# Retention's products with q in the tiles of v, and the squares of norm 2 behind two K tiles of fill

## The chip, the cores and the metric

The kernel runs on one core of a Trainium2 chip. The metric is the device time of one execution in microseconds; the time before the change is the median of three runs. A profiled execution was taken beside them.

## The reference

One step of a decoder trunk with one layer: 256 prompt positions and 8 samples of one position each share the weights, 264 columns in all. Everything is float32, and the model dimension is 2048.

```
h = rmsnorm(x, norm1_g) * (1 + scale1) + shift1
q, k, v, gr, u, ga, gb = split(h @ w_in)        # q, k rotated; 8 heads, dqk 256, dv 512
# retention of a sample, head by head, with its own state S (256 x 512):
S_new = gamma_h * S + outer(k, v)               # an output
o     = q @ S_new
y_a = (group_norm(o) * gn_g * silu(gr)) @ w_proj_a
mixed = sigmoid(ga) * y_a + sigmoid(gb) * y_b   # y_b: pooled branch
x = x + gate1 * (mixed @ w_out)
h2 = rmsnorm(x, norm2_g) * (1 + scale2) + shift2
x = x + gate2 * ((silu(a) * b) @ w_down)        # a, b: causal conv of h2 @ w_up
```

The six shifts, scales and gates are one product each of silu(c) with w_mod ("modulation"). The prompt's retention is done with scores and a state of its own. A final norm follows.

## The kernel before, in words

**Weights.** All weights stream from memory once. A chunk is 4 K tiles of 128 by 256 outputs (512 KB). SP's queue loads it into a ring of six raw tiles (L203), ScalarE casts it to `whi` (L214), VectorE subtracts to get the remainder `wlo` (L215), each in a ring of three, and TensorE runs 24 products: hi with hi, hi with lo, lo with hi (L228 to L236). These products go through `mm` (L194), which ties every product behind the one before it, so from the end of the start stage on their order on TensorE is the order written in the program. Everything else is laid out by the framework's planner, which simulates a timeline and gives each engine one list of instructions. `behind(a, b)` (L183) tells the planner alone that a comes after b on their engine.

**A head.** While the chunks of head h+1 run (q, k, then half of the output projection of head h-1, v, the other half, v, gate), the retention of head h is spread between them: `main` has 32 chunks (24 in head 0; in head 7 the gate ga takes the place of the next head), and `spread` (L90) puts step j of n behind chunk ceil(32(j+1)/n). Before the change there are 18 steps: rows of v, scores, values and keys; samples 0 and 1; prompt outputs; samples 2 and 3; prompt states; samples 4 and 5; modulation with the first sums; samples 6 and 7; modulation with the second sums; sample outputs, centring, gate. The first sums so come behind chunk 22 and the second behind chunk 27 (16 and 20 in head 0).

**A sample** (`sample`, L652): GpSimd's queue loads S (512 KB, ring of four, shared in head 7 with the stores of ga); VectorE's shuffle spreads the row of v over the partitions into `vb` (ring of two); ScalarE scales S by gamma; VectorE adds k times v in two halves; GpSimd's queue stores S. The product with q goes to a tile of its own, `qt` (ring of four): ScalarE multiplies half 0 by q (L665), VectorE adds half 1 (L666). `sample_q` (L670) sums over the partitions on TensorE for four samples at a time, with products of 32 columns at four tile positions. One step of modulation, which loads four raw tiles of 512 KB on SP's queue and runs eight products, goes in front of each.

**Norm 2.** The output projection ends with its eighth group (L850). Squares of the groups 0 to 6 are summed and enter the norm's sum `pn_n2` early; the squares of the last two tiles (`square_part`, L791) are taken behind their residual and enter it by two products that are not tied. Nine K tiles of a modulation product (`gt2`, L854, four products each, weights loaded ahead) are the fill while the norm is worked out: square root on ScalarE, reciprocal over 264 columns on VectorE (L341), the samples' columns of h2 by three GpSimd products and a split, the prompt's by VectorE and ScalarE tile by tile (`modulated`, L344). Then the up projection starts.

Of the kernel before, what the change touches and what calls it, by code (L numbers as in the profile page):

```python
# [20 lines left out]
F32 = mybir.dt.float32  # L21
# [4 lines left out]
P = 128  # L26
# [3 lines left out]
TP = 256  # L30
NS = 8
T = TP + NS
H = 8
DQK = 256
DV = 512
# [51 lines left out]
GAMMA = constants()[3]  # L87
# [13 lines left out]
def run(steps):  # L101
    for step in steps:
        step()


def call(f, *args):
    return lambda: f(*args)


def together(*steps):  # L110
    return lambda: run(steps)
# [18 lines left out]
def build(ctx, tc, a):  # L130
    nc = tc.nc
    ve, sc, te, sy, gp = nc.vector, nc.scalar, nc.tensor, nc.sync, nc.gpsimd
# [50 lines left out]
    def behind(ins, first):  # L183

        tc.add_manual_dep(ins.ins, first.ins.name, mybir.DependencyInfo(
            mybir.DependencyClass.NoSync, mybir.DependencyReason.DATA), reason="issue order")


    mark = {}
# [21 lines left out]
    def split_loaded(w, name, nk):  # L211
        hi = wts.tile([P, 4, 256], F32R, tag="whi", name=f"wh_{name}", bufs=3)[:, 0:nk, :]
        lo = wts.tile([P, 4, 256], F32R, tag="wlo", name=f"wl_{name}", bufs=3)[:, 0:nk, :]
        c = sc.copy(out=hi, in_=w)  # L214
        t = ve.tensor_tensor(out=lo, in0=w, in1=hi.bitcast(F32), op=ALU.subtract)  # L215
        if name == "st0_0":
            behind(c, mark["ms"])
            behind(t, mark["hm"])
        if name == "st0_4":
            behind(c, mark["hi"])  # L220
            behind(t, mark["lo"])
        return hi, lo
# [114 lines left out]
    def rstd_from(pn, name):  # L337

        r = keep.tile([P, T], F32, tag="rstd", name=f"rstd_{name}")
        mark[name] = sc.activation(out=r, in_=pn[:, :T], func=AF.Sqrt, bias=eps[:, 0:1], scale=1.0 / D)  # L340
        ve.reciprocal(out=r, in_=r)  # L341
        return r

    def modulated(x, r, isc, ish, k0, nk, xh, xl, name):  # L344
# [228 lines left out]
    def retention(h, mods):  # L573

        q, k, v, gr = raw_q[h], raw_k[h], raw_v[h], raw_gr[h]
        st = {}
# [75 lines left out]
        def sample(b):  # L652

            s = hp.tile([P, 2, DV], F32, tag="S", name=f"S{h}_{b}", bufs=4)
            gp.dma_start(out=s, in_=a["state_ret"][b, h].rearrange("(d p) v -> p d v", p=P))
            vb = hp.tile([P, DV], F32, tag="vb", name=f"vb{h}_{b}", bufs=2)
            ve.stream_shuffle(out=vb, in_=st["vsr"], mask=[b] * 32)
            sc.mul(out=s, in_=s, mul=GAMMA[h])
            for d in range(2):
                ve.scalar_tensor_tensor(out=s[:, d, :], in0=vb, scalar=k[:, d, TP + b:TP + b + 1],  # L660
                                        in1=s[:, d, :], op0=ALU.mult, op1=ALU.add)
            gp.dma_start(out=a["rs"][b, h].rearrange("(d p) v -> p d v", p=P), in_=s)

            t = hp.tile([P, DV], F32, tag="qt", name=f"qt{h}_{b}", bufs=4)
            sc.mul(out=t, in_=s[:, 0, :], mul=q[:, 0, TP + b:TP + b + 1])  # L665
            ve.scalar_tensor_tensor(out=t, in0=s[:, 1, :], scalar=q[:, 1, TP + b:TP + b + 1], in1=t,  # L666
                                    op0=ALU.mult, op1=ALU.add)
            st["qt", b] = t

        def sample_q(half):  # L670

# [33 lines left out]
        def gate():  # L705
# [16 lines left out]
            sample_rows, scores, together(call(values, 0), call(values, 1), keys),  # L722
            call(sample, 0), call(sample, 1), together(call(prompt_out, 0), call(prompt_out, 1)),
            call(sample, 2), call(sample, 3), together(call(prompt_state, 0), call(prompt_state, 1)),
            call(sample, 4), call(sample, 5), together(*mods[0:1], call(sample_q, 0)), call(sample, 6),
            call(sample, 7), together(*mods[1:2], call(sample_q, 1)),
            sample_out, centre, gate,
        ]

# [61 lines left out]
    def square_part(kt, b, dst, pool, norm, t0, t1):  # L791

        q = pool.tile([P, T], F32, tag="t1", name=f"rql_{norm}_{b}_{t0}", bufs=2)[:, 0:t1 - t0]
        sc.activation(out=q, in_=dst[:, kt, t0:t1], func=AF.Square)
        te.matmul(out=pns[norm][:, t0:t1], lhsT=ones, rhs=q, start=False, stop=b == 1, skip_group_check=t0 > 0)

    def residual(acc, xin, gate, g, dst, pool, norm):

        for b in range(2):
            residual_part(acc, xin, gate, 2 * g + b, b, dst, 0, T)  # L800
            if g == 7:
                square_part(2 * g + b, b, dst, pool, norm, 0, T)
        k = slice(2 * g, 2 * g + 2)
        if g == 0:
            sums[norm] = pool.tile([P, 2, T], F32, tag="ssum", name=f"ssum_{norm}", bufs=1)
            sc.activation(out=sums[norm], in_=dst[:, k, :], func=AF.Square)
        elif g < 7:
            q = pool.tile([P, 2, T], F32, tag="t2", name=f"rsq_{norm}_{g}", bufs=4)
            sc.activation(out=q, in_=dst[:, k, :], func=AF.Square)
            ve.tensor_tensor(out=sums[norm], in0=sums[norm], in1=q, op=ALU.add)  # L810
        if g == 6:
            warm_sqrt(norm, sums[norm][:, 0, 0:1])
            pns[norm] = psx(f"pn_{norm}")
            for b in range(2):
                te.matmul(out=pns[norm][:, :T], lhsT=ones, rhs=sums[norm][:, b, :], start=b == 0, stop=False)

    sums, pns = {}, {}
    x1 = midp.tile([P, KT, T], F32, tag="ya", name="x1")
    with tc.tile_pool(name="res", bufs=2) as rp:
        def load_ahead(src, name):  # L820
            return loaded.pop(0)

        loaded = []

        def loads_ahead(g):

            for n in range(2):
                w = rp.tile([P, 4, 256], F32, tag="rawx", name=f"wm2_ahead_{g}_{n}", bufs=KT)
                if g > 1:
                    hold(w[:, 0, 0:1], x1[:, 2 * g - 3, 0:1])  # L830
                gp.dma_start(out=w, in_=a["w_mod2"][2 * (GT2 - 2) + n, g])
                loaded.append(w)

        c_late = rp.tile([P, KT, 32], F32, tag="c_late", name="c_late", bufs=1)
        gt2, _ = mod2_steps(GT2)
        xbs = {}

        def load_x(g):
            xbs[g] = rp.tile([P, 2, T], F32, tag="xb", name=f"xb{g}")
            sy.dma_start(out=xbs[g], in_=a["xT"][:, 2 * g:2 * g + 2, :])  # L840

        def use_wo(g, acc):
            residual(acc, xbs[g], GT1, g, x1, rp, "n2")
            sy.dma_start(out=dram["x1"][:, 2 * g:2 * g + 2, :], in_=x1[:, 2 * g:2 * g + 2, :])

        for gs in ([0, 1], [2], [3], [4], [5], [6], [7]):
            for g in gs:
                load_x(g)
                loads_ahead(g)
            run(gemm(a["w_out"], gs, m_hi, m_lo, KT, "wo", use_wo, apart=gs == [7]))  # L850

        hold(c_late[:, 0, 0:1], x1[:, 12, 0:1])
        gp.tensor_copy(out=c_late, in_=csil)
        for kt in range(9):  # L854
            gt2(kt, 1, load_ahead if kt < KT // 2 else raw_chunk, c_late)
        r2 = rstd_from(pns["n2"], "n2")
    h2_hi = acts.tile([P, KT, T], F32R, tag="a_hi", name="h2_hi")
# [187 lines left out]
```

## Time and profile before

| | before |
|---|---|
| median of 3 runs (lowest to highest), us | 2294.38 (2294.06 to 2294.73) |
| profiled execution: its own time / its span, us | 2300.14 / 2298.4 |
| mean granted TensorE clock | 0.993 |
| TensorE busy / VectorE / ScalarE / GpSimd | 98% / 65% / 47% / 9% |
| read and written, over the span | 243 GB/s |

The span goes from the first to the last instruction of the profiled execution; times in the rows are from the span's start. Busy times count instructions that run; a matmul overlaps the next one, so a busy TensorE is not one at its peak. An instruction's idle time before it is in brackets, with what ended it.

### The profile page before, as it was taken

How to read it: one execution, taken by the hardware profiler on the slowest of the kernel's cores; microseconds unless marked ns; L12 is line 12 of the kernel's file. 1: busy time of each engine (PE TensorE's matmuls, PEld its weight loads, DVE VectorE, ACT ScalarE, POOL GpSimd, SP SyncE). 2: the span in 40 equal slices, each digit the busy share in tenths (PEclk: the TensorE clock that was granted, in tenths of full speed). 3: DMA queues.
4: the chain of work that ended last, by engine and by line, in shares of the span. 5: the costliest groups of instructions: out<-in, count | busy, mean ns of one | idle time of the engine just before them, and what ended most of it. 6: DMA issues, size and time to landing. Idle time of an engine off the chain costs nothing. (4 is left out here: it accounts for less than half of the span.)

```text
span 2298.4 us, 44797 instructions
## 1 busy us (share of the span) xinstructions
PE 2252.8 (98%) x18432; PEld 2148.8 (93%) x18432; DVE 1504.3 (65%) x2152; ACT 1088.6 (47%) x1364; POOL 218.2 (9%) x386
## 2 busy tenths in 40 slices
PE   8999999999999999999999999999999999999998
PEld 6898998898999999999999989989999999999998
DVE  6666676585758686867676568576666666654444
ACT  4333354355554545454545454454444444444343
POOL 0000222011101010101010101111000010000000
PEclk9999999999999999999999999999999999999999
DMA  9777867897877787878787879856666666666662
GB/s 334 246 263 268 278 193 264 296 343 285 283 257 272 255 286 257 294 260 298 240 294 238 285 229 347 301 164 186 199 183 214 192 207 212 184 191 190 187 193 98
DMA packets 168253, 561.13 MB, mean 244 GB/s; under 512 B 18448, under 2 KB 28752, under 8 KB 168048
## 3 DMA queue, kind: packets, MB, share of 16 engines
q1 hardware_dynamic: 144048, 474.08, 62.4%
q0 software_dynamic: 23568, 83.73, 10.1%
q8 instruction: 144, 2.36, 0.4%
q10 hardware_dynamic: 432, 0.46, 0.1%
q14 instruction: 61, 0.50, 0.1%
HBM read 509.82 MB, written 48.38 MB: 243 GB/s over the span
## 5 line engine op out<-in xcount | busy, mean ns | idle before, releaser
L196 PE MATMUL acc_up<-h_hi,wh_up 128*128 128x264 f32 x1408 | 400.8, 285 | 1.5 <-ACT h_hi L225 1.5
L196 PE MATMUL acc_up<-h_lo,wh_up 128*128 128x264 f32 x1408 | 400.1, 284 | 0.7 <-DVE h_lo L226 0.7
L196 PE MATMUL acc_up<-h_hi,wl_up 128*128 128x264 f32 x1408 | 399.6, 284 | 0.0
L196 PE MATMUL acc_in<-h_hi,wh_in 128*128 128x264 f32 x1344 | 390.3, 290 | 3.2 <-ACT wh_in L214 3.2
L196 PE MATMUL acc_in<-h_hi,wl_in 128*128 128x264 f32 x1344 | 384.6, 286 | 6.8 <-DVE wl_in L215 6.8
L196 PE MATMUL acc_in<-h_lo,wh_in 128*128 128x264 f32 x1344 | 384.7, 286 | 0.0
L215 DVE TENSOR_TENSOR wl_up<-w_up,wh_up 128x1024 fp32r<-128x1024 f32 x176 | 216.0, 1227 | 182.0 <-ACT wh_up L214 181.9
L215 DVE TENSOR_TENSOR wl_in<-w_in,wh_in 128x1024 fp32r<-128x1024 f32 x168 | 207.6, 1237 | 154.6 <-ACT wh_in L214 154.6
L214 ACT CAST wh_up<-w_up 128x1024 fp32r<-128x1024 f32 x176 | 184.6, 1049 | 252.3 <-issue 148.7
L214 ACT CAST wh_in<-w_in 128x1024 fp32r<-128x1024 f32 x168 | 175.7, 1048 | 207.9 <-PE acc_in L196 79.4
L196 PEld LDWEIGHTS acc_in<-h_hi,wh_in 128*128 128x128 f32 x1344 | 255.4, 190 | 17.3 <-ACT wh_in L214 13.5
L196 PEld LDWEIGHTS acc_up<-h_hi,wh_up 128*128 128x128 f32 x1408 | 265.4, 189 | 5.8 <-ACT h_hi L225 2.5
L196 PEld LDWEIGHTS acc_up<-h_lo,wh_up 128*128 128x128 f32 x1408 | 265.7, 189 | 0.9 <-DVE h_lo L226 0.9
L196 PEld LDWEIGHTS acc_up<-h_hi,wl_up 128*128 128x128 f32 x1408 | 265.0, 188 | 0.0
L196 PEld LDWEIGHTS acc_in<-h_hi,wl_in 128*128 128x128 f32 x1344 | 254.8, 190 | 9.2 <-DVE wl_in L215 9.1
L196 PEld LDWEIGHTS acc_in<-h_lo,wh_in 128*128 128x128 f32 x1344 | 255.5, 190 | 0.5
L196 PE MATMUL acc_st<-h_hi,wh_st 128*128 128x264 f32 x704 | 202.1, 288 | 1.0 <-ACT h_hi L358 1.0
L196 PE MATMUL acc_st<-h_hi,wl_st 128*128 128x264 f32 x704 | 200.4, 286 | 1.9 <-DVE wl_st L215 1.8
L196 PE MATMUL acc_st<-h_lo,wh_st 128*128 128x264 f32 x704 | 200.2, 285 | 0.0
L196 PE MATMUL acc_dn<-f_lo,wh_dn 128*128 128x264 f32 x680 | 192.9, 284 | 0.0
L196 PE MATMUL acc_dn<-f_hi,wl_dn 128*128 128x264 f32 x680 | 192.8, 284 | 0.0
L196 PE MATMUL acc_dn<-f_hi,wh_dn 128*128 128x264 f32 x680 | 192.8, 284 | 0.0
(262 smaller groups left out, 5346.4 us busy)
## 6 DMA issues: line engine op xcount, KB each, us to landing
wm<-in_w_mod SPq DMA_DIRECT2D x176, 512.0 KB, 6.3
w_up<-in_w_up SPq DMA_DIRECT2D x176, 512.0 KB, 3.7
w_in<-in_w_in SPq DMA_DIRECT2D x168, 512.0 KB, 4.9
w_dn<-in_w_down SPq DMA_DIRECT2D x88, 512.0 KB, 3.6
S<-in_state_ret POOLq DMA_DIRECT2D x64, 512.0 KB, 7.0
out_rs<-S POOLq DMA_DIRECT2D x64, 512.0 KB, 5.6
w_pa<-in_w_proj_a SPq DMA_DIRECT2D x64, 512.0 KB, 4.2
w_st<-in_w_in SPq DMA_DIRECT2D x66, 384.0 KB, 4.5
```

Of the source, the lines that this page charges most:

```text
L196: ins = te.matmul(**kw)
L214: c = sc.copy(out=hi, in_=w)
L215: t = ve.tensor_tensor(out=lo, in0=w, in1=hi.bitcast(F32), op=ALU.subtract)
```

## The change

- The product with q is written into the sample's `vb` tile; the ring of `vb` has six tiles, and `qt` is gone (six tiles in both).
- The shuffle and the scaling of S are tied behind the subtraction and the cast of the latest split in front of them in the program.
- The first sums, with their step of modulation, stand behind sample 4 instead of sample 5; an empty step stands in front of the second sums, so there are 19 steps. The first sums come behind chunk 19 (14 in head 0), the second behind chunk 27 (21 in head 0), samples 0 to 7 behind chunks 7, 9, 12, 14, 17, 21, 22 and 24 (before: 8, 9, 13, 15, 18, 20, 24 and 25).
- The last squares of norm 2 are taken in the program behind two K tiles of the fill, and their two products go through `mm`.
- Norm 2's reciprocal is done in two parts, the eight columns of the samples first.

```diff
@@ -213,6 +213,7 @@
         lo = wts.tile([P, 4, 256], F32R, tag="wlo", name=f"wl_{name}", bufs=3)[:, 0:nk, :]
         c = sc.copy(out=hi, in_=w)
         t = ve.tensor_tensor(out=lo, in0=w, in1=hi.bitcast(F32), op=ALU.subtract)
+        mark["split"] = c, t
         if name == "st0_0":
             behind(c, mark["ms"])
             behind(t, mark["hm"])
@@ -338,7 +339,9 @@
 
         r = keep.tile([P, T], F32, tag="rstd", name=f"rstd_{name}")
         mark[name] = sc.activation(out=r, in_=pn[:, :T], func=AF.Sqrt, bias=eps[:, 0:1], scale=1.0 / D)
-        ve.reciprocal(out=r, in_=r)
+
+        for t in (slice(TP, T), slice(0, TP)) if name == "n2" else (slice(0, T),):
+            ve.reciprocal(out=r[:, t], in_=r[:, t])
         return r
 
     def modulated(x, r, isc, ish, k0, nk, xh, xl, name):
@@ -653,19 +656,19 @@
 
             s = hp.tile([P, 2, DV], F32, tag="S", name=f"S{h}_{b}", bufs=4)
             gp.dma_start(out=s, in_=a["state_ret"][b, h].rearrange("(d p) v -> p d v", p=P))
-            vb = hp.tile([P, DV], F32, tag="vb", name=f"vb{h}_{b}", bufs=2)
-            ve.stream_shuffle(out=vb, in_=st["vsr"], mask=[b] * 32)
-            sc.mul(out=s, in_=s, mul=GAMMA[h])
+            vb = hp.tile([P, DV], F32, tag="vb", name=f"vb{h}_{b}", bufs=6)
+
+            behind(ve.stream_shuffle(out=vb, in_=st["vsr"], mask=[b] * 32), mark["split"][1])
+            behind(sc.mul(out=s, in_=s, mul=GAMMA[h]), mark["split"][0])
             for d in range(2):
                 ve.scalar_tensor_tensor(out=s[:, d, :], in0=vb, scalar=k[:, d, TP + b:TP + b + 1],
                                         in1=s[:, d, :], op0=ALU.mult, op1=ALU.add)
             gp.dma_start(out=a["rs"][b, h].rearrange("(d p) v -> p d v", p=P), in_=s)
 
-            t = hp.tile([P, DV], F32, tag="qt", name=f"qt{h}_{b}", bufs=4)
-            sc.mul(out=t, in_=s[:, 0, :], mul=q[:, 0, TP + b:TP + b + 1])
-            ve.scalar_tensor_tensor(out=t, in0=s[:, 1, :], scalar=q[:, 1, TP + b:TP + b + 1], in1=t,
+            sc.mul(out=vb, in_=s[:, 0, :], mul=q[:, 0, TP + b:TP + b + 1])
+            ve.scalar_tensor_tensor(out=vb, in0=s[:, 1, :], scalar=q[:, 1, TP + b:TP + b + 1], in1=vb,
                                     op0=ALU.mult, op1=ALU.add)
-            st["qt", b] = t
+            st["qt", b] = vb
 
         def sample_q(half):
 
@@ -722,8 +725,8 @@
             sample_rows, scores, together(call(values, 0), call(values, 1), keys),
             call(sample, 0), call(sample, 1), together(call(prompt_out, 0), call(prompt_out, 1)),
             call(sample, 2), call(sample, 3), together(call(prompt_state, 0), call(prompt_state, 1)),
-            call(sample, 4), call(sample, 5), together(*mods[0:1], call(sample_q, 0)), call(sample, 6),
-            call(sample, 7), together(*mods[1:2], call(sample_q, 1)),
+            call(sample, 4), together(*mods[0:1], call(sample_q, 0)), call(sample, 5), call(sample, 6),
+            call(sample, 7), together(), together(*mods[1:2], call(sample_q, 1)),
             sample_out, centre, gate,
         ]
 
@@ -792,14 +795,15 @@
 
         q = pool.tile([P, T], F32, tag="t1", name=f"rql_{norm}_{b}_{t0}", bufs=2)[:, 0:t1 - t0]
         sc.activation(out=q, in_=dst[:, kt, t0:t1], func=AF.Square)
-        te.matmul(out=pns[norm][:, t0:t1], lhsT=ones, rhs=q, start=False, stop=b == 1, skip_group_check=t0 > 0)
+        (mm if norm == "n2" else te.matmul)(
+            out=pns[norm][:, t0:t1], lhsT=ones, rhs=q, start=False, stop=b == 1, skip_group_check=t0 > 0)
 
     def residual(acc, xin, gate, g, dst, pool, norm):
 
         for b in range(2):
             residual_part(acc, xin, gate, 2 * g + b, b, dst, 0, T)
             if g == 7:
-                square_part(2 * g + b, b, dst, pool, norm, 0, T)
+                squares.append(call(square_part, 2 * g + b, b, dst, pool, norm, 0, T))
         k = slice(2 * g, 2 * g + 2)
         if g == 0:
             sums[norm] = pool.tile([P, 2, T], F32, tag="ssum", name=f"ssum_{norm}", bufs=1)
@@ -814,7 +818,7 @@
             for b in range(2):
                 te.matmul(out=pns[norm][:, :T], lhsT=ones, rhs=sums[norm][:, b, :], start=b == 0, stop=False)
 
-    sums, pns = {}, {}
+    sums, pns, squares = {}, {}, []
     x1 = midp.tile([P, KT, T], F32, tag="ya", name="x1")
     with tc.tile_pool(name="res", bufs=2) as rp:
         def load_ahead(src, name):
@@ -852,6 +856,9 @@
         hold(c_late[:, 0, 0:1], x1[:, 12, 0:1])
         gp.tensor_copy(out=c_late, in_=csil)
         for kt in range(9):
+            if kt == 2:
+                run(squares)
+                squares.clear()
             gt2(kt, 1, load_ahead if kt < KT // 2 else raw_chunk, c_late)
         r2 = rstd_from(pns["n2"], "n2")
     h2_hi = acts.tile([P, KT, T], F32R, tag="a_hi", name="h2_hi")
```

## Rows read from the trace of the kernel before

**Rows 1.** The page, busy time of TensorE: us (share) xinstructions.

```profile
PE 2252.8 (98%) x18432; PEld 2148.8 (93%) x18432; DVE 1504.3 (65%) x2152; ACT 1088.6 (47%) x1364; POOL 218.2 (9%) x386
```

**Rows 2.** TensorE's waits, 475 to 562 us: total us, times, longest.

```profile
PE mean_mu L693 <- DVE s_mu L691: 1.6, 1, 1.6
PE acc_in L196 <- DVE wl_in L215: 1.2, 2, 0.7
PE osp L684 <- ACT qs L679: 0.8, 1, 0.8
```

**Rows 3.** TensorE's waits, 562 to 1228 us.

```profile
PE acc_in L196 <- DVE wl_in L215: 4.9, 7, 0.8
PE acc_in L196 <- ACT wh_in L214: 1.8, 2, 1.1
```

**Rows 4.** TensorE's waits, 1228 to 1372 us.

```profile
PE qp L196 <- DVE qt L666: 3.5, 1, 3.5
```

**Rows 5.** Windows: us, PE PEld DVE ACT POOL (x), granted clock, DMA share, GB/s.

```profile
546.00:554.00 8.00, 6.91 (x31) 6.23 (x32) 7.07 (x11) 4.89 (x6) 0.00 (x0) 0.57 0.82 287
1102.00:1107.00 5.00, 5.00 (x30) 5.00 (x31) 2.45 (x2) 2.62 (x4) 0.00 (x0) 0.66 0.86 293
1327.00:1335.00 8.00, 6.76 (x24) 4.25 (x23) 4.18 (x6) 3.06 (x5) 0.72 (x1) 0.57 1.00 370
1501.00:1506.00 5.00, 4.03 (x20) 3.83 (x21) 5.00 (x14) 2.68 (x7) 0.00 (x0) 0.66 0.52 204
```

**Rows 6.** Timeline of ScalarE, from 1098.55: start, length, instruction, idle before it.

```profile
1098.55 1.06 ACT L658 ACTIVATE S<-S 128x1024 f32<-128x1024 f32 x1 [1.55 <-DMA S<-in_state_ret]
1099.52 1.03 ACT L214 CAST wh_in<-w_in 128x1024 fp32r<-128x1024 f32 x1
```

**Rows 7.** The tiles of S, who waited for them: us, times.

```profile
  ACT wh_in L214: 9.3, 7
```

**Rows 8.** The tiles qt: min/median/max ns, first and last start; what they waited for.

```profile
L665 ACT ACTIVATE qt<-S,q x64: 705/718/738, 486.3 to 1327.3; 128x512 f32<-128x512 f32 x64
...
  PE qp L196: 5.4, 7
```

**Rows 9.** Transfers, 624 to 634 (first row), then 640 to 650: KB, us to landing.

```profile
w_in<-in_w_in SPq DMA_DIRECT2D x3, 512.0 KB, 3.7
...
DMA packets 1075, 3.95 MB, mean 395 GB/s; under 512 B 111, under 2 KB 111, under 8 KB 1074
...
w_in<-in_w_in SPq DMA_DIRECT2D x2, 512.0 KB, 9.5
```

**Rows 10.** Windows, columns as in rows 5.

```profile
600.00:612.00 12.00, 12.00 (x98) 11.84 (x98) 10.26 (x16) 4.96 (x7) 2.72 (x4) 1.00 0.93 312
684.00:720.00 36.00, 36.00 (x285) 34.92 (x284) 36.00 (x65) 18.96 (x25) 7.69 (x11) 1.00 0.73 248
```

**Rows 11.** Timeline of ScalarE in head 7, at 1321.84.

```profile
1321.84 1.04 ACT L214 CAST wh_ga<-w_ga 128x1024 fp32r<-128x1024 f32 x1 [7.90 <-DMA w_ga<-in_w_in]
```

**Rows 12.** Timeline of norm 2, from 1490.61.

```profile
1490.61 4.50 PE L196 MATMUL mp<-wm_ahead,c_late 128*32 128x512 f32 x40
...
1491.38 0.17 DVE L789 TENSOR_TENSOR x<-x,xb 128x8 f32<-128x8 f32 x1
1491.55 0.73 ACT L794 ACTIVATE rql_n<-x 128x264 f32<-128x264 f32 x2
...
1495.03 1.16 PE L795 MATMUL pn_n<-rql_n,ones 128*128 128x264 f32 x4
...
1496.23 0.48 ACT L340 ACTIVATE rstd_n<-pn_n,eps 128x264 f32<-128x264 f32 x1 [3.95 <-PE pn_n L795]
1496.74 1.80 DVE L341 RECIPROCAL rstd_n<-rstd_n 128x264 f32<-128x264 f32 x1 [3.84 <-ACT rstd_n L340]
...
1501.31 0.39 PE L196 MATMUL acc_up<-h_hi,wh_up 128*128 128x264 f32 x1 [1.54 <-ACT h_hi L225]
...
1502.36 0.59 PE L196 MATMUL acc_up<-h_lo,wh_up 128*128 128x264 f32 x1 [0.67 <-DVE h_lo L226]
```

## The prediction

> **What bounds the kernel now.** I read the page's busy times first: TensorE is busy for 98% of the span [rows 1]. There is no slower engine to relieve; the change can only take away TensorE's idle time, and the time at the lower clock that follows it. So the second view is TensorE's waits, stage by stage, and the third the granted clock around the longest of them. The chain of waits tells the same: from norm 2 on it is nearly all matmuls.
>
> The eight heads run from 475 to 1372 us. In head 0 TensorE waits 1.6 us for the sums of the mean, 1.2 us for remainders of weights and 0.8 us for the copy in front of the transposes [rows 2]. In heads 1 to 6 it waits 4.9 us (7 times) for remainders and 1.8 us (twice) for casts of weights [rows 3]. In head 7 it waits 3.5 us for one product with q [rows 4]. The clock was granted at 0.57 for 8 us in head 0, at 0.66 for 5 us in head 5, at 0.57 for 8 us in head 7 and at 0.66 for 5 us at norm 2 [rows 5]. Each begins just after a cluster of these waits; the two levels are 1.2 and 2.4 GHz, and a stretch of w us at a granted share c loses w(1-c): 3.4, 1.7, 3.4 and 1.7 us.
>
> Why the weights are late is on ScalarE, not in the transfer of weights. At 1098.55 a scaling of a sample's state S starts, after 1.55 us of waiting for that S to land, and only behind it, at 1099.52, the cast of the weights for which TensorE then stands idle [rows 6]. These are the next head's samples 0 to 3, which the planner put into the end of this head, far ahead of their use. All over the run casts of wh_in had 9.3 us of idle ended by an instruction on S in front of them, 7 times [rows 7]. Their products of samples 4 to 7 wait 5.4 us (7 times) on ScalarE for the first half of the sums on TensorE, since the ring of product tiles holds four [rows 8]; so the S tiles come free only then, and four loads of S start at once, in the same stretch as 2 MB of modulation weights. There a load of w_in lands after 9.5 us, against 3.7 us ten microseconds earlier [rows 9].
>
> **The change, part by part.** No matmul, and no instruction per sample, goes or comes; one reciprocal is split.
>
> (a) Six tiles for v and product. Products of samples 4 and 5 lose the wait for the first sums; those of 6 and 7 now wait for them earlier, at the shuffle that fills the tile. The product on ScalarE (0.72 us) now overwrites v, so it waits for both sums into S instead of the first, and VectorE's second half of it for that [rows 8].
>
> (b) The first half of the sums, with one step of modulation, goes from behind chunk 22 of 32 to behind chunk 19 (head 0: 16 to 14 of 24); the second stays behind 27 (head 0: 20 to 21). The step issues four loads of 512 KB on SP's queue, so they pass in front of the loads of three chunks; the two bursts are eight chunks apart instead of five. At chunk 19 the first four products are long done: they lie before the second group of projections.
>
> (c) The ties. The scaling of S stays behind the cast of the chunk in front of it in the program, the shuffle behind its subtraction. The next head's scalings can't be put in front of this head's casts any more. That is what each stall above needs. What it costs: ScalarE gets them, 4 x 1.06 us, in the stretch where VectorE is full (36.00 of 36 us) but ScalarE has 18.96 of 36 us busy [rows 10]; it fits. Behind a tied shuffle that waits for the first sums stand VectorE's next subtractions. Sample 6 comes behind chunk 22, whose weights can be split only when TensorE has left chunk 19 (three buffers), just ahead of the sums; so the wait is short, and the next subtraction is needed two chunks later.
>
> Gains in the heads. Head 0: 1.6 + 1.2 + 0.8 less 0.8, because sums and transposes are now one chunk apart and the copy between them can still show, plus 3.4 of clock: 6.2 us. Heads 1 to 6: 4.9 + 1.8 + 1.7 of clock = 8.4 us. Head 7: ends 0 and 3.5 + 3.4 = 6.9 us. There the cast itself started only at 1321.84, after 7.90 us in which ScalarE waited for its transfer [rows 11], and the tiles of S are shared with the gate's stores, whose order in the ring changes; the nearest row is that wait for a transfer, which the change doesn't shorten for sure, so I take half, 3.4.
>
> New waits can't be read here. They end below at 0 (nothing more to gain: TensorE has no idle in the full stretch) and above at one short stall per head, as the longest of those seen for weights, 0.75 us, by eight heads: 6.0 us. As VectorE has no spare time there, and the waits of (a) fall on it, I take the upper end, 6.0.
>
> (d) Norm 2. TensorE's fill starts at 1490.61: 40 instructions, then the sums of the last squares at 1495.03, then the rest of it, and idle from 1499.77 to 1501.31 (1.54 us) and again 0.67 us before 1502.36 [rows 12]. With the sums behind 16 of the fill: 16 x 4.42/40 = 1.77 us, so 1492.38. The squares are done at 1491.55 + 0.73 = 1492.28, just in time. Square root after the same 1.20 us, at 1493.58, 0.48 long; the first 8 columns of the reciprocal, between nothing and the 0.17 us of VectorE's eight-column sum (I take 0.17), then 256/264 of 1.80: end near 1496.0 instead of 1498.54. From there to the first product of h_lo took 3.82 us, so 1499.8; the fill, which is the same work, ends at 1499.77. GpSimd's products for the samples, which need only the 8 columns, start before the rest of the reciprocal instead of behind it, so there is some margin. Gain 1.54 + 0.67 + 1.7 of clock = 3.9 us, ends 0 and 3.9. The cover is the fill; were the sums still late, it would be spent and the idle would stay.
>
> Sum: 6.2 + 8.4 + 3.4 + 3.9 - 6.0 = 15.9 us. On the profiled execution: span 2298.4 to 2282.5, its own time 2300.14 to 2284.2. The runs' median is 5.8 us below that execution; I take the difference over as it is: 2294.38 - 15.9 = 2278.5 us.
>
> **A rule against it.** At 600 to 612 us, where samples 4 and 5 will release their S tiles, the transfers are already at 0.93 of the engines [rows 10]. What follows is a mechanism of this kernel: two loads of S of 512 KB come into that stretch, 1.3 us each at the 395 GB/s of the full stretch that starts at 640, 2.6 us in 12 us of which 0.84 us is free; weights behind them come up to 1.8 us later. The Trainium skill, "DMA: Bandwidth & Descriptors", section "Issuing engines are not separate DMA queues", says that transfers started by different engines run on the same 16 DMA engines and interleave; by that rule a load taken out of one full stretch is only a gain if it goes to an emptier one, and the 9.5 against 3.7 us above agree with it.
>
> **Rivals.**
> *The loads stall elsewhere.* 1.8 us in each of seven heads that load ahead is 12.6 us in place of the 6.0 above: 2278.5 + 6.6 = 2285.1. For it: the 0.93. Against it: TensorE had no idle at 600 to 612, so the weights had a lead.
> *The heads come out even.* The planner lays out all four queues anew. If it pays for each stall with another, only norm 2 is left: 2294.38 - 3.9 = 2290.5, which counts as no change. For it: the stalls are short (most 0.75 us) and many. Against it: they share one cause that the tie forbids. That norm 2 keeps its wait too would give 2294.4, also no change.
> *VectorE stands at every product.* By (a) it must wait for ScalarE's 0.72 us plus the handing over, 0.8 us, unless the planner has other work to put between. In the full stretch such a stand passes into the weights and so to TensorE: with six samples 6 x 0.8 x 8 heads = 38.4 us against 21.9 us of gains: 2294.4 + 16.5 = 2310.9. It makes the kernel slower from (21.9 + 4.6)/(8 x 0.8) = 4.1 stands per head on. For it: 36.00 of 36. Against it: the queue holds other samples' work to put between, and samples 5 to 7 are tied to chunks behind the full stretch.
>
> **How the numbers follow.** Forecast 0.60, loads 0.15, even 0.15, VectorE 0.10. A measurement of this kernel tells 0.2%, 4.6 us, from no change. Faster by more: the first two and a little of the third, 0.78; within: 0.13; slower: 0.09. The range's lower end takes all of head 7 and no new waits: 2278.5 - 3.5 - 6.0 = 2269.0; the upper end covers the loads and most of the even case: 2291.
>
> **What would show it.** Right: no scaling of S that waits for a landing between the two groups of sums; S loads in two groups per head; no idle of TensorE behind the second sums; full clock in heads 0 and 5; at norm 2 the sums at 1492.4 relative to the fill's start at 1490.6, and no idle before the up projection. Wrong: VectorE waiting for ScalarE's product in the full stretch, the weights' subtractions late there, or the sums of samples 6 and 7 late at chunk 27 in head 7. It would be wrong as a whole if idle of equal length appeared inside the heads at other chunks.

## The result and the profile after

The changed kernel takes 2264.11 us (median of 4 runs, 2261.48 to 2270.32); the kernel before, on the same chip, took 2294.56 us (4 runs, 2294.06 to 2296.78). The ratio is 0.9862, with a 95% interval of 0.9845 to 0.9878: 30.5 us faster, about twice the 15.9 us of the forecast, and below the lower end of its range.

The profiled execution took 2261.48 us. From its page, the span and the busy times, to be set against [rows 1]:

```profile
span 2259.7 us, 44874 instructions
...
PE 2234.2 (99%) x18432; PEld 2140.0 (95%) x18432; DVE 1505.0 (67%) x2153; ACT 1089.6 (48%) x1364; POOL 222.5 (10%) x386
```

The work is the same (VectorE has one instruction more, the split reciprocal); TensorE's idle time went. The next rows, from the views of three tiles after the change, are the first and last products of a stage; their last columns before the shapes are the first and last start.

```profile
L587 PE MATMUL vsp<-cst,vsc x32: 270/272/273, 470.5 to 1216.0; 128*128 128x128 f32 x32
...
L196 PE MATMUL acc_wo<-m_hi,wh_wo x256: 281/284/477, 1362.3 to 1456.1; 128*128 128x264 f32 x128
...
L196 PE MATMUL acc_up<-h_hi,wh_up x1408: 281/284/391, 1465.6 to 1984.8; 128*128 128x264 f32 x176
```

Heads with their tail, from the first `vsp` to the first `acc_wo`, take 1362.3 - 470.5 = 891.8 us; the same view of the kernel before has 475.1 and 1396.4, so 921.3: 29.5 us less. The rest of the way, from the output projection's end to the up projection's, is 3.9 us shorter (532.6 to 528.7). The output and down projections did not change (94.0 and 264.9 us both times). The start stage was 4.6 us shorter in this execution; the change does not touch it, and it took 473.8 to 477.4 us in the eleven other traces in which it is unchanged, so that part is spread between executions. (The two profiled executions differ by 38.7 us, the medians by 30.5: that of before lies 5.6 us above its median, that of after, the fastest of its four, 2.6 below.)

One execution gives the time of the heads to no better than 5 or 6 us. With the same order of instructions on every engine, the old heads take 915.4 us in the trace of `e1_norm2_alone` (921.3 above), and the new ones 896.9 us in that of `e2_heads_alone` (891.8 above), there with 4.5 us of listed waits and one stretch at half clock.

TensorE's waits after, over all heads (470 to 1362 us), against [rows 2 to 4]:

```profile
PE acc_in L196 <- DVE wl_in L215: 1.0, 2, 0.8
PE acc_pa L196 <- DVE y_a L742: 0.9, 2, 0.5
```

That is the whole list: 1.9 us, where the same view of before, over the heads and their tail (475 to 1397 us), adds up to 17.3. Two lines of that view are in no row of the forecast, though they lie in the window of [rows 4]:

```profile
PE mt L326 <- ACT ms L323: 1.1, 1, 1.1
...
PE acc_ga L196 <- DVE y_a L739: 0.6, 1, 0.6
```

Windows after, columns as in [rows 5], near the places that answer to it. The fifth answers to the one in [rows 10] with VectorE's 36.00 us: both begin 0.7 us behind the start of head 2, which is at 683.3 us before and at 670.2 us after. The last is the one in which the forecast feared the loads of S:

```profile
540.00:548.00 8.00, 8.00 (x68) 7.37 (x60) 4.70 (x7) 4.62 (x5) 0.00 (x0) 1.00 0.98 371
1078.00:1083.00 5.00, 5.00 (x46) 3.26 (x39) 1.54 (x2) 0.87 (x3) 0.00 (x0) 1.00 0.81 277
1297.00:1305.00 8.00, 8.00 (x68) 7.29 (x61) 2.95 (x4) 3.58 (x6) 0.00 (x0) 1.00 0.97 361
1465.00:1470.00 5.00, 5.00 (x44) 4.35 (x37) 5.00 (x14) 3.95 (x8) 0.00 (x0) 1.00 0.61 205
670.90:706.90 36.00, 36.00 (x291) 35.53 (x291) 33.47 (x55) 22.11 (x28) 5.61 (x8) 1.00 0.71 232
598.00:610.00 12.00, 12.00 (x99) 11.88 (x98) 7.17 (x9) 6.41 (x8) 2.18 (x4) 1.00 0.90 288
```

The clock is granted in full in all four places where it had fallen. VectorE has 33.47 us of work in the stretch where it had 36.00: it is still nearly full, and TensorE has no idle there. And the transfers have 0.90 of their engines at 598 to 610 us, but TensorE is busy throughout.

VectorE's waits for ScalarE's product with q, from 470 to 1362 us after; before, they are 4.8 us (4 times):

```profile
DVE vb L669 <- ACT vb L668: 3.4, 4, 0.9
```

The heads with their tail as one window, before and after:

```profile
475.10:1396.40 921.30, 903.89 (x7227) 853.74 (x7226) 656.24 (x902) 486.46 (x569) 101.74 (x147) 0.99 0.80 273
470.50:1362.30 891.80, 889.72 (x7226) 848.01 (x7225) 658.42 (x902) 487.67 (x569) 102.41 (x147) 1.00 0.82 282
```

Of the 29.5 us in the heads, 17.3 - 1.9 = 15.4 are listed waits and 8.5 the half clock [rows 5]; the remaining 5.6 stand in no list of waits: they are part of the 14.2 us by which TensorE's busy time fell.

The forecast's sign of two groups of loads of S per head did not come. Before, four of them start behind the first sums at once (640.0 to 642.2 us); now they start one by one (at 687.7, 690.4, 701.8, 712.5 us in head 2).

ScalarE's waits late in head 7 after the change (1260 to 1305 us), where the transfers of `w_ga` in the kernel before (1290 to 1335 us) cost it 21.1 us, 5 times, up to the 7.90 of [rows 11]:

```profile
ACT wh_ga L214 <- PE acc_ga L196: 10.9, 6, 2.8
ACT wh_ga L214 <- DMA w_ga<-in_w_in: 5.8, 4, 2.3
```

Here ScalarE now waits mostly for TensorE, not for weights: they are ahead.

ScalarE in head 5 after the change, where [rows 6] had the scaling of S between its wait and the cast:

```profile
1076.10 2.17 ACT L214 CAST wh_in<-w_in 128x1024 fp32r<-128x1024 f32 x2 [5.73 <-DMA w_in<-in_w_in]
1080.38 0.59 ACT L682 COPY qs<-qp 128x512 f32<-128x512 f32 x1 [2.12 <-PE qp L196]
1082.98 1.05 ACT L214 CAST wh_in<-w_in 128x1024 fp32r<-128x1024 f32 x1 [2.01 <-DMA w_in<-in_w_in]
```

The casts now wait for the weights' own transfers, 5.73 us here, and no scaling stands in front. ScalarE has that time; TensorE has no idle here.

Norm 2 after, the timeline that answers to [rows 12]:

```profile
1456.56 1.92 PE L196 MATMUL mp<-wm_ahead,c_late 128*32 128x512 f32 x16
...
1458.41 1.16 PE L196 MATMUL pn_n<-rql_n,ones 128*128 128x264 f32 x4
...
1459.50 5.36 PE L196 MATMUL mp<-wm_ahead,c_late 128*32 128x512 f32 x48
1459.61 0.48 ACT L341 ACTIVATE rstd_n<-pn_n,eps 128x264 f32<-128x264 f32 x1 [1.37 <-PE pn_n L196]
1460.12 1.82 DVE L344 RECIPROCAL rstd_n<-rstd_n 128x8 f32<-128x8 f32 x2 [1.26 <-ACT rstd_n L341]
...
1464.68 1.04 PE L196 MATMUL mp<-wm,c_late 128*32 128x512 f32 x8
1465.65 0.39 PE L196 MATMUL acc_up<-h_hi,wh_up 128*128 128x264 f32 x1
1465.88 0.28 PE L196 MATMUL acc_up<-h_lo,wh_up 128*128 128x264 f32 x1
```

The sums stand 1.85 us behind the fill's start, as forecast (1.77), the two reciprocals together take 1.82 us (one took 1.80), and the first product of the up projection carries no idle in front.

### The profile page after: what moved, and what is told of

Its sections match the earlier page's. It is cut to its first block, busy times and chain, and to the rows that moved or that the text cites. A ratio compares the mean times of both kernels' runs of the same rounds, so it can differ in the third digit from the quotient of the medians.

```text
span 2259.7 us, 44874 instructions
## 1 busy us (share of the span) xinstructions
PE 2234.2 (99%) x18432; PEld 2140.0 (95%) x18432; DVE 1505.0 (67%) x2153; ACT 1089.6 (48%) x1364; POOL 222.5 (10%) x386
## 3 DMA queue, kind: packets, MB, share of 16 engines
q0 software_dynamic: 23568, 83.73, 10.5%
## 4 chain that ended last, share of the span: by engine, by line
PE 60%; DVE 1%; DMA 1%; issue 0%; ACT 0%; SPq 0%; DVEq 0%; ACTq 0%
PE acc_up L196 23%; PE acc_dn L196 11%; PE acc_in L196 10%; PE acc_pa L196 4%; PE acc_wo L196 4%; PE acc_ga L196 4%; PE mp L196 1%; PE acc_dn L948 1%; DMA w_in<-in_w_in 1%; PE qp L196 0%; PE scp L598 0%; DMA sgr<-sga_scratch 0%; DVE wl_in L215 0%; DVE wl_pa L215 0%; PE sp L648 0%
## 5 line engine op out<-in xcount | busy, mean ns | idle before, releaser
L215 DVE TENSOR_TENSOR wl_up<-w_up,wh_up 128x1024 fp32r<-128x1024 f32 x176 | 216.1, 1228 | 181.2 <-ACT wh_up L214 180.9
```

## The experiments

Each was timed beside the kernel before; differences named without a partner are against that one. Two parts of the change alone first, then the ties, the move, the tiles, and a try at more.

**Norm 2 alone** (`e1_norm2_alone`): the kernel before, with only part (d).

```diff
+        for t in (slice(TP, T), slice(0, TP)) if name == "n2" else (slice(0, T),):
+            ve.reciprocal(out=r[:, t], in_=r[:, t])
...
+                squares.append(call(square_part, 2 * g + b, b, dst, pool, norm, 0, T))
...
+            if kt == 2:
+                run(squares)
```

> Norm 2's part alone on the kernel before. Theory (norm 2 and the heads are independent; norm 2 is worth its idle and the clock after it): 2294.5 - 3.9 = 2290.6 us, no idle of TensorE between the fill and the up projection, full clock there, the heads' waits as before. Rival (the heads gave the whole 30.5 us and the sums of the squares only move idle): 2294.5 us, idle of 1 to 2 us left behind the fill.

Measured: 2291.62 us against 2295.19, ratio 0.9987 (0.9979 to 0.9996), 3.6 us less. The stretch from the output projection to the up projection's end takes 528.7 us, as in the changed kernel.

**All but norm 2** (`e2_heads_alone`): the changed kernel without those lines.

> The heads' three edits (tiles, move, ties) without norm 2's. Theory: the rest of the 30.5 us, 2294.5 - 26.6 = 2268 us, with 1.5 + 0.7 us of idle and a stretch at half clock at norm 2 as before. Rival (norm 2 carries more than its idle, since the planner lays out everything anew): 2275 us or more.

Measured: 2269.08 us, 0.9892 (0.9878 to 0.9906), 26.1 us less; the heads take 896.9 us. TensorE's waits at norm 2 are back as in [rows 12]:

```profile
PE acc_up L196 <- ACT h_hi L226: 1.5, 1, 1.5
PE acc_up L196 <- DVE h_lo L227: 0.7, 1, 0.7
```

The two parts add up: 3.6 + 26.1 = 29.7 of 30.5 us.

**The ties alone** (`e3_ties_alone`), on the kernel before. The forecast gave them what it gave the heads.

```diff
+        mark["split"] = c, t
...
+            behind(ve.stream_shuffle(out=vb, in_=st["vsr"], mask=[b] * 32), mark["split"][1])
+            behind(sc.mul(out=s, in_=s, mul=GAMMA[h]), mark["split"][0])
```

> The two ties alone: products with q keep their own four tiles, the first sums stay behind sample 5. Theory (scalings of S in front of casts on ScalarE make the stalls): the stalls behind the second sums of heads 0 to 5 go, while four loads of S still start at once behind the first sums and the products of samples 4 to 7 still wait for them: 2294.5 - 15 = 2279 us (2274 to 2284). Rival (the six tiles and the moved sums do it by spreading the loads; the ties are an extra): 2291 us or more.

Measured: 2288.32 us against 2295.19, 0.9975 (0.9964 to 0.9986): 6.9 us less, not 15. ScalarE's waits for transfers of weights and of S in the kernel before, from 585 to 1228 us:

```profile
ACT wh_in L214 <- DMA w_in<-in_w_in: 41.3, 19, 3.6
ACT S L658 <- DMA S<-in_state_ret: 41.1, 25, 3.7
```

In this kernel, from 585 to 1220 us, no scaling waits for a landing, and the casts wait for their own weights instead:

```profile
ACT wh_in L214 <- DMA w_in<-in_w_in: 90.4, 34, 9.5
```

One line of ScalarE's timeline in head 4 of this kernel:

```profile
980.87 1.04 ACT L214 CAST wh_in<-w_in 128x1024 fp32r<-128x1024 f32 x1 [9.54 <-DMA w_in<-in_w_in]
```

So there are two causes in series, and the ties take away only the first: what the scalings waited before, the casts wait now.

**No ties** (`e4_no_ties`): the changed kernel with both `behind` taken off.

> The changed kernel without its two ties: six tiles, first sums behind sample 4, norm 2's part. Theory: the planner puts the next head's scalings in front of this head's casts again; norm 2's 3.9 us and a little from the spread loads stay: 2294.5 - 8 = 2286 us (2281 to 2291). Rival (tiles and move do it): within 4 us of the changed kernel, 2265 to 2268 us.

Measured: 2295.49 us, 0.9997 (0.9988 to 1.0006), with norm 2's 3.6 us still in: the heads as a whole gain nothing (921.5 us in its trace). By the table below, head 7 gains its 10 us even so, and heads 2 to 6 lose 13. VectorE's timeline in head 2, where [rows 10] call it full, shows what comes in there:

```profile
685.20 0.73 DVE L661 STREAM_SHUFFLE vb<-vsr 128x512 f32<-128x512 f32 x1
...
688.79 0.77 DVE L661 STREAM_SHUFFLE vb<-vsr 128x512 f32<-128x512 f32 x1
689.89 1.23 DVE L215 TENSOR_TENSOR wl_in<-w_in,wh_in 128x1024 fp32r<-128x1024 f32 x1
691.37 4.07 DVE L664 SCALAR_TENSOR_TENSOR S<-vb,k,S 128x512 f32<-128x512 f32 x6
695.35 1.23 DVE L215 TENSOR_TENSOR wl_in<-w_in,wh_in 128x1024 fp32r<-128x1024 f32 x1
```

With six tiles free, the planner puts six shuffles in a row (the first and last are shown) and six halves of sums after them; one subtraction of weights fits in ten microseconds. TensorE's waits in this kernel:

```profile
PE acc_in L196 <- DVE wl_in L215: 17.1, 14, 2.3
```

Before, these waits were 6.1 us (9 times).

**Each tie off alone** (`e7_no_dve_tie`, `e8_no_act_tie`): the shuffle untied, then the scaling untied.

```diff
-            behind(ve.stream_shuffle(out=vb, in_=st["vsr"], mask=[b] * 32), mark["split"][1])
+            ve.stream_shuffle(out=vb, in_=st["vsr"], mask=[b] * 32)
```

> The changed kernel without the tie of the shuffle; the scaling stays tied. Theory (with six tiles free the planner packs six shuffles into VectorE's full stretch, which costs 2.3 us of idle in each of five heads and led the kernel without ties back to 2295): the packing comes back, about 2264 + 8 heads x 2 = 2278 us (2272 to 2284). Rival (only ScalarE's scalings matter): 2264 to 2267 us.

```diff
-            behind(sc.mul(out=s, in_=s, mul=GAMMA[h]), mark["split"][0])
+            sc.mul(out=s, in_=s, mul=GAMMA[h])
```

> The changed kernel without the tie of the scaling; the shuffle stays tied. Theory: scalings of the next head's samples 0 and 1 are packed early again, but their loads land early too, so their wait is short; sample 2 and 3 block casts behind the second sums: 2264 + 8 = 2272 us (2267 to 2278). Rival (the shuffle's tie alone does it): 2264 to 2266 us.

Measured without the shuffle's tie: 2272.44 us, 0.9897 (0.9882 to 0.9913), 8 us above the changed kernel; the six shuffles are packed again, from 683.35 to 686.92, and remainders are late 12 times, 5.4 us. Without the scaling's tie: 2325.40 us, 1.0133 (1.0117 to 1.0148), 30 us slower than before the change. That was far off what I expected. ScalarE's timeline in head 2 of this kernel:

```profile
733.56 1.06 ACT L662 ACTIVATE S<-S 128x1024 f32<-128x1024 f32 x1 [9.11 <-DMA S<-in_state_ret]
734.52 1.03 ACT L214 CAST wh_pa<-w_pa 128x1024 fp32r<-128x1024 f32 x1
735.46 0.72 ACT L668 ACTIVATE vb<-S,q 128x512 f32<-128x512 f32 x1
736.08 1.03 ACT L214 CAST wh_pa<-w_pa 128x1024 fp32r<-128x1024 f32 x1
737.02 0.59 ACT L568 COPY v<-acc_in 128x528 f32<-128x528 f32 x1
```

A scaling stands 9.11 us for its S, and behind it, in order, stand casts and the copy of an accumulator. TensorE's waits:

```profile
PE acc_pa L196 <- ACT v L568: 22.6, 6, 5.0
...
PE sp L648 <- ACT o L641: 12.1, 5, 4.2
```

From 585 to 1280 us the scalings wait 132.6 us (36 times) for landings. The changed kernel loses 8 and 61 us with one tie taken off, 31 with both: they do not add. The packed shuffles cost less alone (5.4 us of late remainders) than with both ties off (17.1). Off together, the scalings wait 48.3 us (30 times) in the whole run, less than half; that the untied shuffles hold the sample's chain back and so shield ScalarE is argued, not shown.

**The move taken back** (`e5_no_move`): sums and modulation behind sample 5 again, chunk 22.

```diff
-            call(sample, 4), together(*mods[0:1], call(sample_q, 0)), call(sample, 5), call(sample, 6),
-            call(sample, 7), together(), together(*mods[1:2], call(sample_q, 1)),
+            call(sample, 4), call(sample, 5), together(*mods[0:1], call(sample_q, 0)), call(sample, 6),
+            call(sample, 7), together(*mods[1:2], call(sample_q, 1)),
```

> The changed kernel with the first sums back behind sample 5 (chunk 22) and no empty step. Theory (two causes in series: scalings of S in front of casts, which the ties take away, and behind them the transfer of weights, late where two bursts of modulation weights stand five chunks apart, which the move takes away): casts wait for transfers of w_in behind the second sums as with the ties alone, 0.75 to 2.2 us of idle in most heads: 2264 + 11 = 2275 us (2270 to 2281). Rival (the ties with the six tiles are enough, since S comes free earlier): 2264 to 2268 us.

Measured: 2281.56 us against 2295.37, 0.9945 (0.9931 to 0.9958): 17 us above the changed kernel. ScalarE's waits from 562 to 1216 us in this kernel:

```profile
ACT wh_in L214 <- DMA w_in<-in_w_in: 115.2, 37, 7.2
```

The same view of the changed kernel:

```profile
ACT wh_in L214 <- DMA w_in<-in_w_in: 76.0, 33, 7.0
...
ACT vb L668 <- DVE S L664: 29.5, 29, 2.4
```

With the move the casts wait less for their weights. Two runs tell which half of it counts: **modulation back, sums stay** (`e9_mods_back`), and **sums back, modulation stays** (`e10_sums_back`).

```diff
-            call(sample, 4), together(*mods[0:1], call(sample_q, 0)), call(sample, 5), call(sample, 6),
+            call(sample, 4), call(sample_q, 0), call(sample, 5), together(*mods[0:1], call(sample, 6)),
```

> The changed kernel with the first sums where the change puts them (chunk 19), but their step of modulation back at chunk 22, five chunks ahead of the second one. Theory (of the move's 16 us, the distance of the two bursts of modulation weights is what counts): casts wait for transfers behind the second sums again, 2264 + 13 = 2277 us (2272 to 2282). Rival (the place of the sums counts, as it frees S and the tiles): 2262 to 2268 us.

```diff
-            call(sample, 4), together(*mods[0:1], call(sample_q, 0)), call(sample, 5), call(sample, 6),
+            call(sample, 4), together(*mods[0:1]), call(sample, 5), together(call(sample_q, 0), call(sample, 6)),
```

> The changed kernel with the step of modulation at chunk 19, but the first sums at chunk 22, just in front of sample 6. Then the shuffle of sample 6, tied behind the split of chunk 22, stands on VectorE until the sums that TensorE reaches three chunks later. Theory (the new wait that the forecast priced at 6 us is real and costs nothing only where the sums lie): VectorE waits about 8 us at that shuffle in each head, and TensorE 1 to 3 us behind it: 2264 + 16 = 2280 us (2272 to 2290). Rival (the wait has cover anyway, or the planner moves the shuffle back): 2264 to 2267 us.

Measured with modulation back: 2280.45 us, 0.9935 (0.9923 to 0.9947), 16 us above the changed kernel, as much as with the whole move taken back. A line of ScalarE's timeline in head 1 of this kernel:

```profile
655.66 1.04 ACT L214 CAST wh_in<-w_in 128x1024 fp32r<-128x1024 f32 x1 [7.81 <-DMA w_in<-in_w_in]
```

ScalarE's waits from 562 to 1216 us in it:

```profile
ACT wh_in L214 <- DMA w_in<-in_w_in: 82.9, 36, 8.4
```

So the loss does not go by the casts' waits: they are nearer to the changed kernel's 76.0 than to the 115.2 above.

With the sums back: 2268.08 us, 0.9881 (0.9867 to 0.9895), 4 us above the changed kernel, inside the spread of its runs. My expectation, that the shuffle of sample 6 would hold VectorE until the sums, fell. VectorE's timeline in this kernel:

```profile
736.82 2.35 DVE L215 TENSOR_TENSOR wl_in<-w_in,wh_in 128x1024 fp32r<-128x1024 f32 x2
740.82 0.01 DVE L661 LOAD_MASK_SELECT vb<-vsr  x1 [1.65 <-PE qp L196]
740.82 0.73 DVE L661 STREAM_SHUFFLE vb<-vsr 128x512 f32<-128x512 f32 x1
```

The planner put the subtractions in front, so the shuffle stood 1.65 us and nobody waited for it; over the heads such waits are 10.5 us, 8 times.

The heads by stage, from the first product into `vsp` of one head to that of another (head 7: to the first `acc_wo`), one execution each, us:

| | heads 0 and 1 | heads 2 to 6 | head 7 |
|---|---|---|---|
| before | 208.2 | 556.0 | 157.1 |
| ties alone (`e3_ties_alone`) | 199.2 | 555.7 | 155.8 |
| no ties (`e4_no_ties`) | 205.9 | 568.9 | 146.7 |
| move taken back (`e5_no_move`) | 200.1 | 553.4 | 152.2 |
| modulation back (`e9_mods_back`) | 207.1 | 548.8 | 147.3 |
| sums back (`e10_sums_back`) | 201.3 | 545.9 | 148.5 |
| changed | 199.7 | 545.5 | 146.7 |

The place of the modulation step is worth the 16 us of the medians; that of the sums alone, nothing clear of the spread. Why the place counts is argued, not shown. It sets the distance of the two bursts of modulation weights (eight chunks instead of five), but also what the first burst meets, and no run moved the second one. The two runs with the step at chunk 22 lose at different stages, most in heads 0 and 1 with the sums early and in heads 2 to 7 with the sums late, so one cause for both is not shown either. Loads of S that start together are not it: in head 3 of both runs they start one by one, as in the changed kernel.

**The old tiles** (`e6_old_tiles`): `vb` with two tiles and `qt` with four, the rest as changed.

> The changed kernel with two tiles of v and four of their own for the products. Theory (with ties and move only sample 4's product stands in front of the first sums, so little of S is held): within 4 us of the changed kernel, 2264 to 2268 us, and the products wait for one sum less. Rival (the tiles carry a third of the gain by releasing S): 2272 us or more, four loads of S at once behind the first sums.

Measured: 2266.60 us, 0.9878 (0.9862 to 0.9894), inside the spread of the changed kernel's runs. With the ties and the move in place, part (a) is worth nothing that these runs tell.

**More of the same** (`e11_early_mods`, `e12_early_mods_gp`): since early bursts helped, the modulation steps of the pooled stage, in front of the heads, were put earlier; the second run also moves the stores of `yb` to GpSimd's queue.

```diff
-            run(spread(ahead + prj[wi][:6] + after + prj[wi][6:], gt1[2 * wi:2 * wi + 2]))
+            run(spread(ahead + prj[wi][:6] + after + prj[wi][6:], gt1[2 * wi:2 * wi + 2], 0.7))
```

> The changed kernel with the modulation steps of the stage before the heads spread over 0.7 of each pass instead of the whole, so that no burst of modulation weights stands right in front of the heads' first chunks. If the same cause (a burst in front of loads) makes the 1.6 us of idle at 462 us and the half clock that some executions show after it: 2264 - 2 = 2262 us (2259 to 2264). If those chunks are late because SP waits to issue the stores of the pooled branch: 2264 us, idle unchanged.

```diff
-                sy.dma_start(out=dram["yb"][:, 2 * g:2 * g + 2, :], in_=dst)
+                gp.dma_start(out=dram["yb"][:, 2 * g:2 * g + 2, :], in_=dst)
```

> The run before, and the stores of the pooled branch issued on GpSimd's queue instead of SP's. If SP's order is the cause of the idle at 462 us: 2264 - 3 = 2261 us (2258 to 2263), no idle there. If the burst is: as the run before.

Measured: 2269.92 us (0.9891, 0.9876 to 0.9906) and 2275.59 us (0.9915, 0.9901 to 0.9928), 6 and 11 us above the changed kernel; both misses, the first inside the spread of the changed kernel's runs. In the first the heads take 889.4 us (891.8 in the changed kernel's trace) and the start stage 480.6, where it took 470.5 in that trace and 473.8 to 477.4 in the others. TensorE's waits there, 300 to 475 us:

```profile
PE acc_pb L196 <- DVE ps_lo L500: 3.1, 3, 1.3
PE acc_pb L196 <- ACT wh_pb L214: 1.5, 1, 1.5
```

In the second a cast of `w_pb` waits 9.71 us for its transfer, and the start stage takes 484.9 us. In these two runs, then, the earlier steps cost the pooled stage more than they bring. No run beat the changed kernel.

## Why the forecast was wrong

The direction was right, and the range too high. By its steps, in the two profiled executions:

- **Norm 2, 3.9 us.** Right: 3.9 in the trace, 3.6 by itself. Its 1.7 us of clock do not come in every execution: `e3_ties_alone` has the same two waits there, 1.5 and 0.7 us, and the clock stays at 1.00 (1488 to 1496 us).
- **Head 0, 6.2, and heads 1 to 6, 8.4.** Together 14.6; measured 8.6 in heads 0 and 1 and 10.5 in heads 2 to 6, 19.1 together. All that the forecast listed is gone but 1.0 us of remainders; of the excess of 4.5 us, 3.8 stand in no list of waits, in time that counts as busy, and all of it is within the spread of one execution.
- **"I take the upper end, 6.0" for new waits: the first step that failed.** TensorE's list of waits after is 1.9 us for all heads, and both of its lines stood in the list before (1.0 for remainders where it was 6.1, 0.9 for `acc_pa` where it was 0.8). The reason given was that VectorE has no spare time and that the waits of (a) fall on it. The first half holds: VectorE still has 33.47 of 36 us in that stretch. The second does not. The waits of (a) fall on ScalarE, whose products wait 29.5 us for the sums into S, 29 times from 562 to 1216 us (2.1 us, twice, from 562 to 1228 us before; 15.0 us in `e6_old_tiles`, with tiles of their own). ScalarE has 22.11 of 36 us of work in the full stretch, and TensorE has no idle there. VectorE's waits for those products hardly changed (3.4 us, 4.8 before), and no shuffle waits for the sums. Nor is 0.75 us, from which the 6.0 is made, the longest wait seen for weights: [rows 3] have one of 1.1.
- **"I take half, 3.4" for head 7: the second.** Measured 10.4 us. In the kernel before, TensorE's busy time in eight windows from 1239 to 1397 us is 151.86 of 158.00 us, so 6.1 idle, and 3.4 of half clock: 9.6 in all. Of the waits in its window, 1228 to 1372 us, the forecast took the longest alone and left out 1.1 us in front of the product `mt` and 0.6 in front of `acc_ga`. And it halved what it took, because a cast waited 7.90 us for its transfer [rows 11] and I did not see the change shorten that. It did: the longest such wait there is 2.3 us now. Mostly it is the move that does it: head 7 takes 146.7 us without the ties and, in `e6_old_tiles`, without the six tiles, but 155.8 with the ties alone and 152.2 without the move.

Without these two steps (no new waits, head 7 whole at 6.9) the forecast's own sum is 2294.4 - (6.2 + 8.4 + 6.9 + 3.9) = 2269.0 us, the range's lower end. The 4.9 us still missing are of the size of head 7's rest (3.5) and the excess of heads 0 to 6, and no larger than the difference between two executions of the same heads.

The mechanism was right in half. "Why the weights are late is on ScalarE, not in the transfer of weights" and "They share one cause that the tie forbids" are not so. The ties alone bring 6.9 us of the heads' 26.1, in their trace nearly all of it in heads 0 and 1 (9.0 us by the table); with them casts wait up to 9.54 us for the weights' own transfers. Head 7 gains by the move, without the ties as well. Heads 2 to 6 gain only where both are in, and not in every execution: they take 550.4 us in `e2_heads_alone`, and 551.4 in `e1_norm2_alone` with the old heads. That the move alone brings them nothing is not shown: `e4_no_ties` has the six tiles too, and loses there by the packed shuffles. The row in [rows 7] bears less than was read from it: of the 9.3 us, 7.9 (6 of the 7 times) stand behind products with q, by the view of the tiles `qt`; the scalings' own waits are the 41.1 us above. The forecast had the second cause in hand, the 9.5 against 3.7 us of [rows 9], and used it to explain the loads of S, not to price the move.

The rivals: the loads that stall elsewhere did not, since the stretch from 598 to 610 us has 0.90 of transfers and no idle. The Trainium skill, "DMA: Bandwidth & Descriptors", section "Issuing engines are not separate DMA queues", was named for that rival: it says that transfers run on the same 16 DMA engines and interleave, whichever engine starts them. No run here puts the two queues apart. What the runs do show is of SP's queue: the same four loads three chunks later cost 16 us (`e9_mods_back`). VectorE at every product did not come; a full VectorE with late remainders did, without the ties (17.1 us in `e4_no_ties`), by packed shuffles and not by products. The heads did not come out even.

## What to carry to other kernels

Before pricing a fix for late weights, follow the wait one step past its first cause: if the instruction in front and the transfer behind are both late, one half alone can measure small, as the ties did, and says little about the whole. Read such an experiment stage by stage: one figure for all heads hid that the kernel without ties won 10 us in the last head and lost more in the middle ones. On an engine that works in order, an instruction that waits for a transfer is charged with everything behind it; tie it behind the work that feeds the busiest engine, so that its wait falls into that engine's lead. A full engine does not make every new wait a stall: ask first on which engine the wait falls, and price it against that engine's spare time. And compare windows that begin at the same instruction, not at the same time.

## What the runs showed of the hardware

- Scalings that wait for landings on ScalarE, 36 times and up to 9.11 us, cost 61 us with the same work (`e8_no_act_tie`): TensorE stood for copies of its own accumulators behind it on ScalarE. TensorE's clock was granted at half for long enough there to lose 17 us.
- Four loads of 512 KB issued three chunks later, and so five chunks ahead of four others instead of eight, make the kernel 16 us longer (`e9_mods_back`). The casts' waits for weights from 562 to 1216 us hardly tell it: 82.9 us there, 76.0 in the changed kernel, 115.2 with the sums late as well (`e5_no_move`).
- Gaps of the same lengths did and did not bring the granted clock down. It fell behind 1.54 and 0.67 us at norm 2 [rows 12], and stayed at 1.00 behind the same two in `e3_ties_alone`. It fell behind 0.81 and 0.75 us at 985 to 987 us in `e2_heads_alone` (0.83 from 982 to 992 us), and stayed behind 0.82 and 0.76 us at 462 to 464 us in the changed kernel. Nine microseconds of 32-column products, with the norm's sums among them and no gap, kept it at 1.00 (1456.56 to 1465.65).
- A reciprocal over 8 and then 256 columns took 1.82 us, over 264 at once 1.80 us: the split costs nothing here.
